# Branch A's projection by seven products of quarters, its operand sums by GpSimd in place, x added by accumulating DMA, the first half of the output projection by pairs of token blocks

## The chip, the cores and the metric

The kernel runs on one core of one Trainium2 chip. The core has five engines with queues of their own, each worked off in order: TensorE (PE in the profile; its weight loads are PEld), VectorE (DVE), ScalarE (ACT), GpSimd (POOL) and SyncE (SP). They wait for each other and for transfers through semaphores alone. The metric is the device time of one execution in microseconds (us); lower is better.

## The reference, cut to what matters

One decoder layer on 512 tokens of width 1024, in float32. The last part of it is touched:

```python
ya = ua * sa.reshape(bn, s_len, A_WIDTH) * jax.nn.silu(za)      # branch A, 512 x 1024
yb = o.reshape(bn, s_len, B_WIDTH) * jax.nn.silu(zb)            # branch B, 512 x 1024
merged = jax.nn.sigmoid(ga) * (ya @ w_branch_a[i]) + jax.nn.sigmoid(gb) * (yb @ w_branch_b[i])
mix_out = merged @ w_out[i]
ple = jax.nn.sigmoid(x @ w_ple_gate[i]) * (p[i] @ w_ple[i])
x = layer_norm(DEEPNORM_ALPHA * x + mix_out + ple, ln_g[i], ln_b[i])
```

## The kernel before

Every float32 operand of a matrix product is cut into a high part (the value rounded to float32r, by ScalarE) and a low part (the rest, by VectorE), and each product is three matmuls: high by high, high by low, low by high (`three`, L282). A matmul of the stages named here has a stationary tile of 128x128 and 512 columns (256 in the last block). `later(n, fn)` (L265) puts a piece of work on an agenda that is due n matmuls further on; `product` (L270) records a matmul and then everything due. So the order of work on each engine is written out by numbers counted in matmuls, and no engine holds a time. An engine runs ahead of its place in that order if its data are there.

Weights come as units of 512 KB through a ring of eight raw buffers `wr` (`pump`, L310). `high_part` and `low_part` (L399, L402) cut a unit into `wh` and `wl`, four buffers of each. After its low part, `follow` (L363) either frees the raw buffer, so that SP loads the next unit into it, or lets a GpSimd DMA add another unit to the raw buffer in place (`accum_op`, L375): so a sum of weight blocks is made.

`quad` (L640) computes a 512x1024 by 1024x1024 product as seven products of quarters instead of eight. Each of the seven is 24 matmuls (2 token blocks of 128 rows, 4 blocks of the inner dimension, 3 matmuls), 168 in all, and reads two units of weights or of weight sums; its left operands are quarters of x or yb and four sums of quarters. Between the products ScalarE copies partial results out of PSUM (`keep`, L649) and VectorE adds them (`block`, L653). `token_chunk` (L62) is the plain form: half of the columns, four token blocks side by side in four banks, 96 matmuls, four units.

The order of the stages at the end: gate of the embedding (quad "pg", 168 matmuls), embedding ("ple", 48), branch B's projection (quad "wb", 168, its weight sums for three of the seven products are made earlier in DRAM), **branch A's projection** ("wa", two calls of `token_chunk`, 192), output projection ("out", 192 matmuls for the first half of the columns in a `token_chunk` of 96 and for the second half block by block, 96 with the last token block in two halves). During "wa" the merge runs: the gate `ga` times the projection, plus `mb` (branch B's result times its gate), four transposes by TensorE into a bank (`merge_turn`, L1352), and a cut of that bank into `mh` and `ml`, the operand of "out". `residue` (L1276) loads x in eight pieces and VectorE adds ALPHA times x to `base`, which holds the embedding. `residual` (L1373) adds a bank of "out" to `base` and takes statistics; `last_norm` (L1378) normalises a token block and stores it.

Of the kernel before, what the change touches and what calls it, by code (L numbers as in the profile page):

```python
# [21 lines left out]
P = 128  # L22
D = 1024
T = 512
# [32 lines left out]
BEHIND = (8, 14)  # L57
GELU = 10
# [20 lines left out]
CUT_YB = (0, 4)  # L79
CUT_YA = (4, 8)  # L80
GATES_B = (14, 40, 56, 126)
RESIDUE = (32, 24)
# [28 lines left out]
def token_units(off):  # L111
    return [("t", off + c * T, kk) for c in range(2) for kk in range(4)]
# [23 lines left out]
def plan():  # L136
# [59 lines left out]
    add("wa", "a", token_units(0))  # L196
# [40 lines left out]
def hybrid_layer(ctx: ExitStack, tc: tile.TileContext, a, out: bass.AP):  # L237
# [185 lines left out]
    def next_pair(name, i):  # L423
        u = cursor[0]
        assert STEPS[u][0] == name, (STEPS[u][0], name)
        cursor[0] += 2
        for j in range(4):
            assert u + j in raw, (u, j)
        run(prep(u))
        run(prep(u + 1))  # L430

        pace = BLOCKS / 2 if name == "zq" else 1

        def ask(at, v, fits=lambda chain: True):
            if not pumping and v < len(STEPS) and fits(STEPS[v][2]):
                later(round(at * pace), lambda: run(load(v)))


        for v in range(u + 4, u + 8):
            ask(1, v, lambda chain: chain in ("x", "y"))  # L440
        within = [bool(v < len(STEPS) and STEPS[v][2]) for v in range(u, u + 6)]
        ask(1 if within[2] else 20, u + 6)
        ask(9, u + 5, lambda chain: chain != "b" and chain != "c")
        ask(12, u + 7, lambda chain: chain != "a" and (chain or within[4]))
        for j, at in enumerate(SPLITS.get(name, SPLITS[""])):

            at = BEHIND if i == 5 and j and name not in SPLITS else at
            spread(u + 2 + j, *(round(pace * n) for n in at))
        return split.pop(u), split.pop(u + 1)
# [185 lines left out]
    def operands(h, l, parts):  # L635

        s1, s2, n4, s3 = parts if callable(parts[0]) else [of_sum(parts, c) for c in range(4)]
        return (of_parts(h, l, 0, 0), of_parts(h, l, 4, 0), s1, n4, s2, s3, of_parts(h, l, 4, 2 * P))

    def quad(name, left, banks, place, done, last=None):  # L640
# [46 lines left out]
        for i, (bank, first, after) in enumerate(steps):  # L687
            w = next_pair(name, i)
            if i == 6 and last:
                last()  # L690
# [485 lines left out]
    def rstd_of(st):  # L1176
        mv = small([P, 2], "mv")
        dve.bn_aggr(out=mv, in_=st)
        dve.tensor_scalar(out=mv[:, 1:2], in0=mv[:, 1:2], scalar1=EPS, scalar2=None, op0=OP.add)  # L1179
# [82 lines left out]

    quad("pg", of_x, pairs(False), lambda c, t: base[:, t, c * T:(c + 1) * T], embedding_gate)
# [8 lines left out]
    def embed(c, t, bank):  # L1272
        z = base[:, t, c * T:(c + 1) * T]
        dve.tensor_tensor(out=z, in0=bank, in1=z, op=OP.mult)

    def residue(c, t):  # L1276
        z = base[:, t, c * T:(c + 1) * T]
        x = tmp[0]("x")
        sp.dma_start(out=x, in_=a["x"][t * P:(t + 1) * P, c * T:(c + 1) * T])
        later(20, lambda: dve.scalar_tensor_tensor(out=z, in0=x, scalar=ALPHA, in1=z,  # L1280
                                                   op0=OP.mult, op1=OP.add))

    ybh = big.tile([P, KT, T], F32R, name="ybh", tag="X0")
    ybl = big.tile([P, KT, T], F32R, name="ybl", tag="X1")
    ys = sum_tiles()

    def cut_yb(g, half):
        ts = slice(half * 2 * P, (half + 1) * 2 * P)
        cut(ybh[:, g, ts], ybl[:, g, ts], yb[0][:, g, ts])
# [3 lines left out]
    for i, (g, half) in enumerate([(g, 0) for g in range(KT)] + [(g, 1) for g in range(4, KT)]):  # L1293
        later(CUT_YB[0] + CUT_YB[1] * i, cut_yb, g, half)
    for i, c in enumerate((0, 2, 1, 3)):
        later(4 + 22 * i, load_sum, ys, ysd, c)
# [9 lines left out]

    ya = []

    def cut_ya(g):
        cut(ya[0][:, g, :], ya[1][:, g, :], ua[:, g, :])  # L1310

    def begin_ya():
        ya.extend(post.tile([P, KT, T], F32R, name=n, tag=tag) for n, tag in (("yah", "P0"), ("yal", "P1")))
        for g in range(KT):
            later(CUT_YA[0] + CUT_YA[1] * g, cut_ya, g)
# [11 lines left out]
    def load_gates_b(c, t, tag):  # L1327
        two = late.tile([P, 2, T], F32, name="two", tag=tag)
        gate["gb", c, t], gate["gb", c, t + 1] = two[:, 0, :], two[:, 1, :]
        sp.dma_start(out=two, in_=gates["gb"][t:t + 2, c].rearrange("t p n -> p t n"))  # L1330

    for i, (c, t) in enumerate(((0, 0), (1, 0), (1, 2), (0, 2))):
        later(GATES_B[i], load_gates_b, c, t, "gb"[i % 2])
    quad("wb", operands(ybh, ybl, ys), pairs(True), place_b, mb_done, begin_ya)
    for i in range(8):
        later(RESIDUE[0] + RESIDUE[1] * i, residue, i % 2, i // 2)

    lg = late.tile([P, D], F32, name="lg", tag="g")
    lb = late.tile([P, D], F32, name="lb", tag="b")
    later(100, sp.dma_start, lg, bcast(a["ln_g"], D))  # L1340
    later(130, sp.dma_start, lb, bcast(a["ln_b"], D))

    mh = big.tile([P, KT, T], F32R, name="mh", tag="X0")
    ml = big.tile([P, KT, T], F32R, name="ml", tag="X1")

    def merge(c, t, bank):
        m = gate.pop(("ga", c, t))
        dve.tensor_tensor(out=m, in0=bank, in1=m, op=OP.mult)
        dve.tensor_tensor(out=m, in0=m, in1=mb[0][:, t, c * T:(c + 1) * T], op=OP.add)
        later(12, merge_turn, c, t, m)  # L1350

    def merge_turn(c, t, m):  # L1352
        bank = pp() if c else pbank("sc", 2)
        for j in range(4):
# [3 lines left out]
        act.activation(mh[:, at[0], at[1]], turned, AF.Copy)  # L1358
        dve.tensor_tensor(out=ml[:, at[0], at[1]], in0=turned, in1=mh[:, at[0], at[1]].bitcast(F32),
                          op=OP.subtract)  # L1360
# [12 lines left out]
    def residual(t, piece, n, bank):  # L1373
        z = base[:, t, piece * n:(piece + 1) * n]
        dve.tensor_tensor(out=z, in0=bank, in1=z, op=OP.add)
        dve.bn_stats(out=zst[t][:, piece if n == T else piece - 1, :], in_=z)

    def last_norm(t, cuts):  # L1378
        mv, rs = rstd_of(zst[t])
# [9 lines left out]
    banks = other_banks()  # L1389
    token_chunk(banks, "out", mh, ml)  # L1390
    for t in range(NT):
        later(2 + 6 * t, residual, t, 0, T, banks[t])

    later(RETIRE, pool.drain)
    units = []
    for t in range(NT):
        ts = slice(t * P, (t + 1) * P)
        n = T if t < NT - 1 else T // 2
        for j in range(T // n):
            bank = pp()  # L1400
            for k in range(KT):
                if len(units) <= k // 2:
                    units.append(next_unit("out"))
                h, l = units[k // 2]
                m = slice((k % 2) * T + j * n, (k % 2) * T + (j + 1) * n)
                three(bank[:, :n], mh[:, k, ts], ml[:, k, ts], h[:, m], l[:, m], k == 0, k == KT - 1)
# [44 lines left out]
```

## Time and profile before

| what | us |
|---|---|
| median of three executions (620.26 to 621.1) | 620.74 |
| span of the profiled execution, first to last instruction | 618.3 |
| TensorE busy in that span | 610.0 |
| VectorE busy | 458.8 |
| ScalarE busy | 327.3 |
| GpSimd busy | 108.7 |

The profile gives the profiled execution's span, which is its own time from the first to the last instruction; what lies around it is the difference to the times, about 2.4 us. In a profile row, a group shows its line, engine, operation and tiles, then the count, busy us and mean ns of one, then the idle time before and what ended it. Waits of an engine that is not the last to be ready cost nothing.

### The profile page before, as it was taken

The numbers are of one execution on the slowest core, as the hardware profiler recorded it, in microseconds if no ns is written. First come the engines' busy times: TensorE is split into PE (matmuls) and PEld (weight loads), VectorE is DVE, ScalarE is ACT, GpSimd is POOL, SyncE is SP. The second block draws the span as 40 slices with busy tenths as digits, with TensorE's granted clock in tenths as the row PEclk, the third lists the DMA queues.
The fourth block names the chain that finished last, engine by engine and source line by source line (L and its number), as shares of the span: only waits on it lengthen the run. The fifth ranks groups of instructions, "written<-read, shape, count | busy, mean of one in ns | idle before, by whom it ended". The sixth has DMA issues, their size and how long they took to land.

```text
span 618.3 us, 8634 instructions
## 1 busy us (share of the span) xinstructions
PE 610.0 (99%) x3036; PEld 514.3 (83%) x3036; DVE 458.8 (74%) x800; ACT 327.3 (53%) x528; POOL 108.7 (18%) x120
## 2 busy tenths in 40 slices
PE   9999999999999999999999999999999999999995
PEld 6888888888888888888889988888888888888885
DVE  6996587878878866857578887677657659476486
ACT  6655664655645655478656765456567445232200
POOL 1234021332432620230102120111110010000011
PEclk9999999999999999999999999999999999999999
DMA  8689899679798598689898898999978997753002
GB/s 305 220 244 183 263 301 271 230 206 283 250 268 282 182 281 267 156 271 304 272 308 197 228 247 242 223 249 284 270 207 259 354 270 241 235 193 117 1 34 103
DMA packets 49888, 143.78 MB, mean 233 GB/s; under 512 B 6452, under 2 KB 7604, under 8 KB 49524
## 3 DMA queue, kind: packets, MB, share of 16 engines
q1 hardware_dynamic: 38772, 110.05, 50.4%
q0 software_dynamic: 8192, 28.58, 25.7%
q10 hardware_dynamic: 2880, 4.59, 2.0%
q8 instruction: 24, 0.39, 0.3%
q14 instruction: 20, 0.16, 0.1%
HBM read 120.00 MB, written 34.73 MB: 250 GB/s over the span
## 4 chain that ended last, share of the span: by engine, by line
PE 99%; DVE 0%; issue 0%; DVEq 0%
PE ps_pp L271 56%; PE ps_sc L271 18%; PE ps_tx L271 9%; PE ps_sc L821 3%; PE ps_po L866 3%; PE ps_po L271 3%; PE ps_tr L271 3%; PE ps_tr L855 1%; PE ps_po L475 1%; PE ps_tr L1208 1%; PE ps_po L1208 1%; PE ps_tx L905 0%; PE ps_sc L1355 0%; PE ps_pp L1355 0%; DVE base L1386 0%
## 5 line engine op out<-in xcount | busy, mean ns | idle before, releaser
L403 DVE TENSOR_TENSOR wl<-wr,wh 128x1024 fp32r<-128x1024 f32 (+1 forms) x136 | 166.4, 1227 | 53.8 <-ACT wh L400 53.1
L400 ACT ACTIVATE wh<-wr 128x1024 fp32r<-128x1024 f32 (+1 forms) x136 | 139.9, 1033 | 87.1 <-PE ps_po L271 15.6
L271 PE MATMUL ps_pp<-xh,wh 128*128 128x512 f32 (+1 forms) x276 | 109.5, 397 | 0.0
L271 PE MATMUL ps_pp<-xl,wh 128*128 128x512 f32 (+1 forms) x276 | 107.0, 388 | 0.0
L271 PE MATMUL ps_pp<-xh,wl 128*128 128x512 f32 (+1 forms) x276 | 105.4, 382 | 0.0
L834 ACT ACTIVATE p<-p,sth 128x128 f32<-128x128 f32 (+3 forms) x64 | 35.5, 556 | 47.3 <-DVE sth L832 47.2
L271 PEld LDWEIGHTS ps_pp<-xh,wl 128*128 128x128 f32 x276 | 52.0, 189 | 8.7
L271 PEld LDWEIGHTS ps_pp<-xh,wh 128*128 128x128 f32 x276 | 52.2, 189 | 8.4 <-ACT wh L297 0.5
L271 PEld LDWEIGHTS ps_pp<-xl,wh 128*128 128x128 f32 x276 | 52.2, 189 | 8.3 <-DVE xl L298 0.4
L375 POOL DMA_DIRECT2D wr<-in_w x26 | 22.6, 869 | 156.8 <-DVE wl L403 136.8
L828 DVE CUSTOM_DVE_ANT_0 p<-ps_sc,mask 128x128 f32<-128x128 f32 (+3 forms) x64 | 30.9, 483 | 5.6 <-PE ps_sc L821 5.6
L766 POOL TENSOR_TENSOR hl<-m,hl 128x512 fp32r<-128x512 f32 x16 | 25.1, 1609 | 54.7 <-ACT hl L761 54.7
L271 PE MATMUL ps_pp<-wh,xl 128*128 128x512 f32 x84 | 32.9, 391 | 0.0
L271 PE MATMUL ps_pp<-wl,xh 128*128 128x512 f32 x84 | 32.8, 390 | 0.0
L271 PE MATMUL ps_pp<-wh,xh 128*128 128x512 f32 x84 | 32.7, 389 | 0.0
L271 PE MATMUL ps_sc<-wh,xsh 128*128 128x512 f32 x80 | 31.2, 390 | 0.0
L271 PE MATMUL ps_sc<-wl,xsh 128*128 128x512 f32 x80 | 31.1, 389 | 0.0
L271 PE MATMUL ps_sc<-wh,xsl 128*128 128x512 f32 x80 | 31.1, 389 | 0.0
L1181 POOL TENSOR_TENSOR rs<-mv,mhalf 128x1 f32<-128x1 f32 x8 | 7.7, 961 | 121.6 <-DVE mv L1179 121.6
L271 PE MATMUL ps_pp<-wl,xsh 128*128 128x512 f32 x64 | 25.0, 391 | 0.0
L271 PE MATMUL ps_pp<-wh,xsl 128*128 128x512 f32 x64 | 25.0, 391 | 0.0
L271 PE MATMUL ps_pp<-wh,xsh 128*128 128x512 f32 x64 | 25.0, 390 | 0.0
(365 smaller groups left out, 1389.7 us busy)
## 6 DMA issues: line engine op xcount, KB each, us to landing
wr<-in_w SPq DMA_DIRECT2D x83, 512.0 KB, 4.7
wr<-in_w POOLq DMA_DIRECT2D x22, 512.0 KB, 6.1
k<-hl SPq DMA_DIRECT2D x16, 256.0 KB, 5.2
q<-hl SPq DMA_DIRECT2D x16, 256.0 KB, 4.3
ws_va<-in_w POOLq DMA_DIRECT2D x8, 512.0 KB, 10.9
wr<-ws_va SPq DMA_DIRECT2D x8, 512.0 KB, 4.3
wa<-in_w POOLq DMA_DIRECT2D x6, 512.0 KB, 7.3
kx<-hl SPq DMA_DIRECT2D x12, 256.0 KB, 5.8
```

The lines of the kernel that those rows point to most:

```text
L271: pe.matmul(ps, s, m, start=start, stop=stop, skip_group_check=read_within)
L375: pool.dma_start(out=raw[u][:, :n], in_=weights(STEPS[FOLLOWS[u]][1], n), accum_op=OP.add)
L400: act.activation(h, raw[u][:, :width(STEPS[u][0])], AF.Copy)
L403: dve.tensor_tensor(out=l, in0=raw[u][:, :width(STEPS[u][0])], in1=h.bitcast(F32), op=OP.subtract)
L475: pe.matmul(idle, zeros[:, :P], zeros, start=True, stop=True)
L766: pool.tensor_tensor(out=hl[:, 3 - j, :], in0=m[2 * j], in1=hl[:, j, :].bitcast(F32), op=OP.subtract)
L821: pe.matmul(sc[m][:, :n], q[:, m, i * P:(i + 1) * P], kk[:, m, :n], start=o == 0, stop=o == 1)
L828: dve.tensor_tensor_reduce(out=pr[m][:, :n], in0=sc[m][:, :n], in1=mask[:, T - n:], scale=-(DK ** -0.5), scalar=3e38, op0=OP.add, op1=OP.m ...
L834: act.activation(pr[m][:, :n], pr[m][:, :n], AF.Exp, bias=st[:, m:m + 1], scale=-1.0, accum_out=st[:, 2 + m:3 + m])
L866: pe.matmul(po[:, i * P:(i + 1) * P], at[:, j * P:(j + 1) * P], v[:, j, h * P:(h + 1) * P], start=j == 0, stop=j == i)
L1181: pool.tensor_tensor(out=rs, in0=mv[:, 1:2], in1=mhalf[:, 0:1], op=OP.pow)
L1208: pe.matmul(sa[:, t * P:(t + 1) * P], va[:, t, g * P:(g + 1) * P], aux[0][:, 0, g, :], start=True, stop=True)
```

## The change

**Branch A's projection becomes a `quad`.** It needs the quarters of ya (`ua`) as cut operands, and four sums of them. The sums are made in place: GpSimd subtracts and adds quarters of `ua` (`add_ya`, eight instructions of 128x2x256), and each quarter or sum is cut in two parts (`cut_ya`, 14 cuts in all). The weight sums of "wa" are all made by the chains of accumulating DMAs: eight in place of none, and 14 cuts of units in place of eight. The operands of "pg", "wb" and "wa" now share `xh`, `xl` and the sum tiles, quarter by quarter, as the stage before lets go of them; the sums of yb are loaded during "pg" instead of after it.

**The gates** of both branches are loaded in pairs into two slots of one tile. **x** is added to `base` by four accumulating DMAs of 512 KB on GpSimd's queue. To need no factor on x, `base` holds the sum divided by ALPHA (the embedding and "out" are scaled by 1/ALPHA as they are added; the constant in the norm is EPS / ALPHA ** 2).

**The merge** writes into the tile that `block` made; the addition of `mb` is on GpSimd for token blocks 0 and 1, on VectorE for 2 and 3; transposes go to the banks "tr" and "po". **The first half of "out"** runs token blocks 0 and 1 over all eight blocks of the inner dimension, and then 2 and 3, with four cut units held for both.

```diff
-CUT_YB = (0, 4)
-CUT_YA = (4, 8)
-GATES_B = (14, 40, 56, 126)
-RESIDUE = (32, 24)
+YA22, YA_S1, YA_S3, YA_CUT_S1 = (4, 35), (24, 60), (40, 76), (90, 97)
+YB11, YB12, YB22, LOAD_YS = (28, 43), (52, 59), (170, 177), (76, 100, 124, 148)
...
+GATES = (2, 14, 64, 142, 158, 192, 234, 308)
+OUT_FIRST, OUT_SECOND = (1, 5), (1, 3)
+LAST_NORM = (100, 130)
+MERGE = (24, 15)
+RESIDUE = (180, 36)
...
-    add("wa", "a", token_units(0))
+    quad("wa", "a", token_units(0))
...
+    def add_ya(to, op, x, y, part):
+        (z,), (x,), (y,) = (part_of((ua,), *q, part) for q in (to, x, y))
+        pool.tensor_tensor(out=z, in0=x, in1=y, op=op)
...
+    for n, c in zip(LOAD_YS, (0, 2, 1, 3)):
+        later(n, load_sum, ys, ysd, c)
     quad("pg", of_x, pairs(False), lambda c, t: base[:, t, c * T:(c + 1) * T], embedding_gate)
...
-        dve.tensor_tensor(out=z, in0=bank, in1=z, op=OP.mult)
-
-    def residue(c, t):
-        z = base[:, t, c * T:(c + 1) * T]
-        x = tmp[0]("x")
-        sp.dma_start(out=x, in_=a["x"][t * P:(t + 1) * P, c * T:(c + 1) * T])
-        later(20, lambda: dve.scalar_tensor_tensor(out=z, in0=x, scalar=ALPHA, in1=z,
-                                                   op0=OP.mult, op1=OP.add))
+        dve.scalar_tensor_tensor(out=z, in0=bank, scalar=1.0 / ALPHA, in1=z, op0=OP.mult, op1=OP.mult)
+
+    def residue(t):
+        pool.dma_start(out=base[:, t, :], in_=a["x"][t * P:(t + 1) * P, :], accum_op=OP.add)
...
+    for t in range(NT):
+        later(RESIDUE[0] + RESIDUE[1] * t, residue, t)
+    quad("wb", operands(xh, xl, ys), pairs(True), place_b, mb_done)
...
+    def merge(c, t, z, source):
+        dve.tensor_tensor(out=z, in0=source, in1=gate.pop(("ga", c, t)), op=OP.mult)
+        early = t < NT // 2
+        (pool if early else dve).tensor_tensor(out=z, in0=z, in1=mb[0][:, t, c * T:(c + 1) * T], op=OP.add)
+        later(MERGE[not early], merge_turn, c, t, z)
...
+        bank = pbank("tr" if t % 2 else "po", 1)
...
-    for c in range(2):
-        banks = main_banks() if c else other_banks()
-        for t in range(NT):
-            later(64 + 6 * t, load_gate, "ga", c, t)
-        token_chunk(banks, "wa", ya[0], ya[1])
-        for t in range(NT):
-            later(2 + 6 * t, merge, c, t, banks[t])
+    of_ya = [of_first_sum, of_sum(ys, 1), of_sum(ys, 2), of_sum(ys, 0)]
+    quad("wa", operands(xh, xl, of_ya, 0), pairs(False), lambda c, t: None, merge)
...
-        dve.tensor_tensor(out=z, in0=bank, in1=z, op=OP.add)
+        dve.scalar_tensor_tensor(out=z, in0=bank, scalar=1.0 / ALPHA, in1=z, op0=OP.mult, op1=OP.add)
...
-    banks = other_banks()
-    token_chunk(banks, "out", mh, ml)
...
+    for those in ((0, 1), (2, 3)):
+        banks = {t: pbank("sc", 2) for t in those} if those[0] else {0: pp(), 1: pbank("tx", 1)}
+        for k in range(KT):
...
+            for t in those:
+                ts = slice(t * P, (t + 1) * P)
+                three(banks[t], xh[:, k, ts], xl[:, k, ts], h[:, m], l[:, m], k == 0, k == KT - 1)
```

Three places show what it does to the order on the engines. The line numbers of rows of the changed program are its own: its L382 is L375 before (the accumulating weight DMA), its L410 is L403 (low part of a unit), its L278 is L271 (matmul). On GpSimd's queue, the end of the program before: `wr` with a number is a raw buffer, and the last two DMAs belong to "wb".

```order
L375 DMA wr_4017<-in_w 128x1024
L375 DMA wr_4096<-in_w 128x1024
L375 DMA wr_4685<-in_w 128x1024
L375 DMA wr_4733<-in_w 128x1024
L1181 TENSOR_TENSOR rs<-mv,mhalf 128x1 x4
```

The same queue in the changed program, from the middle of "wa" on: `base<-in_x` is x, and `s<-s,mb` the addition of the merge.

```order
L382 DMA wr_4829<-in_w 128x1024
L382 DMA wr_4858<-in_w 128x1024
L1387 TENSOR_TENSOR s_5090<-s_5090,mb 128x512
L1330 DMA base<-in_x 128x1024
L1387 TENSOR_TENSOR s_5110<-s_5110,mb 128x512
L382 DMA wr_4961<-in_w 128x1024
L382 DMA wr_4991<-in_w 128x1024
L382 DMA wr_4829<-in_w 128x1024
L1330 DMA base<-in_x 128x1024
L382 DMA wr_4858<-in_w 128x1024
L1387 TENSOR_TENSOR s_5262<-s_5262,mb 128x512
```

Where GpSimd had nothing from "wb" to the norms, it now issues weight sums, x and additions in one line; the last weight sum (`wr_4858`, second unit of the seventh product) stands behind the third piece of x.

On VectorE, the second half of "wa" before: a multiplication by the gate and an addition for each bank, with low parts of units between.

```order
L1348 TENSOR_TENSOR gate<-ps_pp,gate 128x512
L1349 TENSOR_TENSOR gate<-gate,mb 128x512
L1348 TENSOR_TENSOR gate<-ps_pp,gate 128x512
L1349 TENSOR_TENSOR gate<-gate,mb 128x512
L403 TENSOR_TENSOR wl<-wr_5122,wh 128x1024
L1359 TENSOR_TENSOR ml<-ps_pp,mh 128x4x128
```

The same engine in the changed program, from the seventh product's first low part: L663 is the sum of `block`, L1385 the gate, L1397 the low part of a turned bank.

```order
L410 TENSOR_TENSOR wl<-wr_4829,wh 128x1024
L1385 TENSOR_TENSOR s_5285<-s_5285,gates 128x512
L663 TENSOR_TENSOR s_5170<-s_5170,ps_pp 128x512
L410 TENSOR_TENSOR wl<-wr_4858,wh 128x1024
L1385 TENSOR_TENSOR s_5170<-s_5170,gates 128x512
L1387 TENSOR_TENSOR s_5170<-s_5170,mb 128x512
L1397 TENSOR_TENSOR xl<-ps_po,xh 128x4x128
L663 TENSOR_TENSOR s_5197<-s_5197,ps_pp 128x512
L1385 TENSOR_TENSOR s_5197<-s_5197,gates 128x512
L1387 TENSOR_TENSOR s_5197<-s_5197,mb 128x512
L410 TENSOR_TENSOR wl<-wr_5008,wh 128x1024
L1397 TENSOR_TENSOR xl<-ps_tr,xh 128x4x128
```

The merge of four banks, with the sums that the quarters need, now stands behind the low part of `wr_4858`.

On TensorE, the changed program in the middle of the seventh product: the transposes of two merged blocks stand between its matmuls.

```order
L278 MATMUL ps_pp<-wl,xh 128x512
L1393 MATMUL ps_tr<-ident,s_5285 128x128 x4
L278 MATMUL ps_pp<-wh,xl 128x512
L1393 MATMUL ps_po<-ident,s_5170 128x128 x4
L278 MATMUL ps_pp<-wh,xh 128x512
```

Before, the transposes of the first half of the columns stood among the matmuls of the second half, and those of the second half among the matmuls of "out".

More of the change, by code (lines that the diff above doesn't have):

```diff
@@ L57 @@
 BEHIND = (8, 14)
+LAST = (7, 11)
 GELU = 10
@@ L1335, in hybrid_layer @@
[L1335 to L1350, printed above, removed]
+    pairs_of_gates = late.tile([P, 2, 2, T], F32, name="gates", tag="R")
@@ L1352, in merge_turn @@
+    later(LAST_NORM[0], load_last, "ln_g", "g")
+    later(LAST_NORM[1], load_last, "ln_b", "b")
+    def merge(c, t, z, source):
[3 more added lines that the diff above has]
+        later(MERGE[not early], merge_turn, c, t, z)
     def merge_turn(c, t, m):
-        bank = pp() if c else pbank("sc", 2)
+        bank = pbank("tr" if t % 2 else "po", 1)
```

123 lines of the change are left out of this document (83 added, 40 removed).

## The prediction

> **What bounds the kernel now.** First I read the page's shares of busy time and its chain, then three stretches from the view by windows, cut at the start of branch B's projection, of branch A's, and of the output projection.
>
> ```profile
> PE 610.0 (99%) x3036; PEld 514.3 (83%) x3036; DVE 458.8 (74%) x800; ACT 327.3 (53%) x528; POOL 108.7 (18%) x120
> PE 99%; DVE 0%; issue 0%; DVEq 0%
> 482.10:520.20 38.10, 38.10 (x170) 31.55 (x169) 26.16 (x32) 19.46 (x23) 1.72 (x2) 1.00 0.91 293
> 520.20:565.60 45.40, 45.40 (x209) 37.62 (x209) 28.78 (x39) 13.38 (x17) 0.00 (x0) 1.00 0.63 214
> 565.60:618.30 52.70, 45.69 (x232) 38.63 (x230) 35.56 (x52) 7.59 (x9) 5.42 (x4) 0.98 0.10 41
> ```
>
> The windows' columns are the length, then busy us of PE, PEld, DVE, ACT and POOL, the granted clock, the DMA share and GB/s. TensorE is the bound: it works through all of the first two stretches, the chain that ends last is 99% its own, and the 7.0 us without it in the third are the last norm and store. So a matmul fewer is worth its full length, if nothing that TensorE now waits for comes late.
>
> **What goes.** The chain in order of time has a piece of 24 matmuls in a row, and it gives the borders of branch A's projection:
>
> ```profile
> 27.00 5.44 PE ps_tr L271 x24
> 517.47 2.72 PE ps_tx L271 x12
> 565.56 1.36 PE ps_sc L271 x6
> ```
>
> A matmul of 512 columns costs 5.44 / 24 = 0.2267 us. Branch A's projection goes from 192 of them to 168: 24 x 0.2267 = **5.44 us less**. Everything else on TensorE keeps its number: 32 transposes, 192 matmuls for the first half of "out" however its blocks are paired. In 520.19 to 565.56 lie 192 matmuls (43.5 us) and 16 transposes, so a set of four costs (45.37 - 43.5) / 4 = 0.46 us. The span would go from 618.3 to 612.9, and the median of 620.74 (2.4 us above the span, for what lies around it) to 615.3.
>
> **What is hidden.** VectorE gains ten cuts of ya in "wb" and loses none of its other work there; an instruction of that size costs 0.69 us, so 6.9 us beside 11.9 us that it has idle in the second window's 38.1. GpSimd's eight additions in place lie where it worked 1.7 us. The eight additions of x leave VectorE:
>
> ```profile
> L1280 DVE SCALAR_TENSOR_TENSOR base<-x,base 128x512 f32<-128x512 f32 x8 | 5.5, 685 | 1.9 <-DMA x<-in_x 1.9
> L907 DVE SCALAR_TENSOR_TENSOR yb<-ps_tx,g,yb x7: 739/750/751, 122.0 to 259.5; 128x512 f32<-128x512 f32 x7
> L1375 DVE TENSOR_TENSOR base<-ps_pp,base x5: 418/691/692, 594.7 to 611.3; 128x512 f32<-128x512 f32 x3, 128x256 f32<-128x256 f32 x2
> ```
>
> These 5.5 us were beside matmuls, so their going is worth nothing. The two-scalar form on a bank costs 0.75 in place of 0.69; behind the last matmul stands one of half the size, at most 0.06 us, which I leave out. The sums of yb (eight transfers of 512 KB) move into "pg". The most delicate transfer there is the last weight sum:
>
> ```profile
> 452.32 0.86 POOL L375 DMA_DIRECT2D wr<-in_w  x1 [0.94 <-DVE wl L403]
> DMA to landing us min/median/max: 6.2/6.2/6.2
> 462.62 1.04 ACT L400 ACTIVATE wh<-wr 128x1024 fp32r<-128x1024 f32 x1
> ```
>
> It landed at 458.5 and was used at 462.6: 4.1 us of cover. Two loads of 512 KB ahead of it cost 3.0 us (below), so I take nothing; without that cover it would be a stall of up to 2 us.
>
> **What is not hidden: the seventh product.** Count from the start of branch A's projection. After product n, TensorE is at 5.44 n, plus 0.46 for each set of transposes passed (after matmuls 63, 75, 137, 149, 150, 162). Two things meet there.
>
> *VectorE's line.* Its pitch, start to start, is shorter than its durations:
>
> ```profile
> 546.84 0.68 DVE L1348 TENSOR_TENSOR gate<-ps_po,gate 128x512 f32<-128x512 f32 x1
> 547.55 0.69 DVE L1349 TENSOR_TENSOR gate<-gate,mb 128x512 f32<-128x512 f32 x1
> 548.16 0.68 DVE L1359 TENSOR_TENSOR ml<-ps_sc,mh 128x512 fp32r<-128x512 f32 x1
> 591.19 1.21 DVE L403 TENSOR_TENSOR wl<-wr,wh 128x1024 fp32r<-128x1024 f32 x1
> 592.32 0.68 DVE L1375 TENSOR_TENSOR base<-ps_po,base 128x512 f32<-128x512 f32 x1
> 506.20 0.39 PE L271 MATMUL ps_pp<-wh,xsl 128*128 128x512 f32 x1
> 506.62 0.60 ACT L651 ACTIVATE s<-ps_pp 128x512 f32<-128x512 f32 x1 [1.66 <-PE ps_pp L271]
> ```
>
> The first number is the start, the second the duration. That is 0.71 after an instruction whose result is read, 0.61 after another, 1.13 after a low part; a copy out of PSUM starts 0.2 after the end of the last matmul's slot and takes 0.6. Product 5 ends at 27.2 + 0.92 = 28.1, its copy at 28.9. Then VectorE does the sum (28.9), the low part of unit 1 (29.5), a gate (30.65), a sum (31.3), and the low part of unit 2 at **31.9**. Call its start D. By the rows in the order, the bank "po" is free for the transposes after matmul 150 when the low part of the turned bank ends, at D + 1.13 + 0.71 + 0.61 + 0.69 = D + 3.1; those after matmul 162 wait for D + 6.9 (four instructions and a low part on); those in the first pair of "out" for the addition that ends at D + 10.0 (two more low parts, a turned bank, a gate). TensorE would reach the last of these, unhindered, at 172 x 0.2267 + 6 x 0.46 = 41.75. So its loss is D - 31.8 from D = 32 on: **0.1 us** with D = 31.9.
>
> GpSimd's addition of the merge, due at 31.35, lies beside that low part. The trace shows such a pair in the attention's stage, where GpSimd subtracts tiles of the same size:
>
> ```profile
> 57.90 2.87 POOL L766 TENSOR_TENSOR hl<-m,hl 128x512 fp32r<-128x512 f32 x2
> 59.41 2.44 DVE L403 TENSOR_TENSOR wl<-wr,wh 128x1024 fp32r<-128x1024 f32 x1 [2.37 <-ACT wh L400]
> L403 DVE TENSOR_TENSOR wl<-wr,wh x136: 948/1219/2445, 19.2 to 591.2; 128x1024 fp32r<-128x1024 f32 x122, 128x768 fp32r<-128x768 f32 x14
> ```
>
> The low part took 2.44 us instead of the median 1.22. I take it that VectorE waits out the 1.6 us addition: D = 33.0, a loss of **1.2 us**.
>
> *The weight sums.* Unit 2 is cut after the last accumulating DMA has landed, and ScalarE needs 1.05 for its high part, so D is at least the landing + 1.05. The rows in the order put five accumulating DMAs in one line ahead of it from the second piece of x on: x, two sums, one sum, x, and then this one. The trace has a line of four, the landings of its first and last, and the slowest pair:
>
> ```profile
> 50.92 0.86 POOL L375 DMA_DIRECT2D wr<-in_w  x1 [2.76 <-DVE wl L403]
> 52.05 0.86 POOL L375 DMA_DIRECT2D wr<-in_w  x1 [0.28 <-DVE wl L403]
> 55.54 0.85 POOL L375 DMA_DIRECT2D wa<-in_w  x1 [2.63 <-DVE wl L403]
> 57.34 0.86 POOL L375 DMA_DIRECT2D wa<-in_w  x1 [0.95 <-DVE wl L403]
> DMA to landing us min/median/max: 6.1/6.1/6.1
> DMA to landing us min/median/max: 7.5/7.5/7.5
> 386.89 0.86 POOL L375 DMA_DIRECT2D wr<-in_w  x1 [0.87 <-DVE wl L403]
> DMA to landing us min/median/max: 9.4/9.4/9.4
> q1 hardware_dynamic: 38772, 110.05, 50.4%
> q0 software_dynamic: 8192, 28.58, 25.7%
> ```
>
> The first landed at 57.0 and the last at 64.8: (64.8 - 57.0) / 3 = 2.6 us each. By the queues' shares of the 618.3 us, GpSimd's queue (q0) takes 25.7% x 618.3 / 28.58 = 5.56 us for a MB, 2.9 us for 512 KB; SP's queue (q1) takes 2.83 us for a MB, 1.5 us for 512 KB. GpSimd issues the second piece of x after the first addition of the merge, which waits for the bank of matmul 36 (8.2) and for VectorE's low part, sum and gate (to 10.9), and takes 1.6: 12.5. It lands 6.2 later, at 18.8. Five more at 2.6 to 2.9 put the last landing at 31.8 to 33.3, D at 32.9 to 34.4, the loss at **1.1 to 2.6 us**. Unit 1 of the same product lands two places earlier, at 26.6 to 27.5, and is cut at 28.1 or later: no loss.
>
> The two causes act on the same D, so they are not added. Between 1.1 and 2.6 I take **1.8 us**, the middle. Its ends for the range are 0 (neither holds) and 6.9 (below).
>
> The sum: -5.44 + 1.8 = -3.6 us; 618.3 becomes 614.7 in span, 620.74 becomes **617.1 us**.
>
> **The rivals.** *All of the gain.* If VectorE loses nothing beside GpSimd and the last sum lands before 30.9 (12.1 us for five, 2.4 each), the time is 615.3. For it: TensorE never waits in the stages before, with the same chains. Against it: the row of 2.44 and the pitch of 2.6.
>
> *Loads share the engines with the sums, and the kernel is slower.* Its place is the landing of the second unit of the seventh product. SP issues four transfers of 512 KB in the time of that line (a pair of gates, ln_g, two units): 4 x 1.5 = 5.9 us. If these go in turn with GpSimd's, the last landing is 31.8 + 5.9 = 37.7, D = 38.75, the loss 6.9 us, the time 620.74 - 5.44 + 6.9 = 622.2. It decides from a landing at 36.2 on (D = 37.25, loss 5.44), which is a pitch of (36.2 - 18.8) / 5 = 3.5 us. For it: the DMA of 386.89 took 9.4 us. Against it, in a stretch with transfers of both queues asked for, the shares of the queues:
>
> ```profile
> q0 software_dynamic: 97, 0.35, 107.1%
> q1 hardware_dynamic: 7, 0.02, 2.5%
> ```
>
> From 442 to 444 us GpSimd's queue had nearly all of the engines and SP's nearly nothing: the loads wait, not the sums. The Trainium skill says otherwise: its page "DMA: Bandwidth & Descriptors", section "SWDGE vs HWDGE vs iDMA", has each DMA engine take its queues in turn, GpSimd's and SP's being different ones. By that rule this rival would be the forecast; the trace of those 2 us does not agree with it, and no run here has both queues full for longer.
>
> *It doesn't do what it says.* The order has 24 rows fewer on TensorE, so the work does go; only waits can take it back.
>
> **How the numbers follow.** The forecast, with a loss from 0.6 to 4.2 us (615.9 to 619.5), has 0.62. All of the gain (below 615.9) has 0.20. The sums late (above 619.5) have 0.18: half of it within 0.2% of the time before, 619.5 to 622.0, which is about what a measurement of this kernel can tell from no change, and half slower. So faster 0.80 (forecast and all the gain, less 0.02 for its edge), same 0.11, slower 0.09. The range goes from 615.3, where there is nothing more to gain, to 620.8, which cuts off some 0.14 of the late cases and a little below.
>
> **What will show it.** The matmuls: the seven products at 38.1 us of TensorE's work, by windows; a longer stretch is waiting. The waits: in the view of waits, TensorE after VectorE at the three sets of transposes, some 1 to 2 us in all, in the seventh product and the first 16 matmuls of "out". VectorE: the low part of the last unit longer than 2 us would show GpSimd's part. The sums: landing times of GpSimd's DMAs of 6 us at first and some 10 for the last; ScalarE's high part of that unit waiting for a DMA. If TensorE waits in "pg", in "wb" or in the second half of "out", the covers above were wrong; if it waits nowhere, the time is 615.3; if the sixth and seventh products both wait for weights, the late case holds.

## The result, and the profile after

The changed kernel took **630.84 us** (median of four executions, 630.05 to 631.1) beside 620.55 us for the kernel before: the ratio is 1.0163, with a 95% interval of 1.0149 to 1.0177. It is slower by some 10 us, where 617.1 was forecast and 620.8 was the top of the range. The page of its profile, with the lines that answer to those shown of before:

```profile
span 629.1 us, 8655 instructions
PE 610.4 (97%) x3012; PEld 511.4 (81%) x3012; DVE 474.4 (75%) x800; ACT 337.9 (54%) x540; POOL 139.7 (22%) x144
...
PE 82%; DMA 7%; issue 5%; DVE 3%; ACT 1%; POOL 1%; DVEq 0%; POOLq 0%; ACTq 0%
```

The 24 matmuls are gone (3012 rows for 3036). But TensorE is idle for 18.7 us of the span instead of 8.3, and the chain that ended last, which was its own from end to end, now runs through DMA, other engines and the time to issue for a sixth of it. Its share of busy time, 97%, hides this; the busy time even includes matmuls at half the clock, as seen below.

The view by windows, cut where the first matmuls of branch B's projection, branch A's and the output projection start (columns: length, busy us and count of PE, PEld, DVE, ACT, POOL, then granted clock, DMA share, GB/s):

```profile
484.30:524.40 40.10, 38.89 (x170) 31.22 (x169) 33.42 (x36) 22.75 (x30) 9.70 (x8) 1.00 0.69 208
524.40:576.60 52.20, 44.95 (x193) 35.79 (x192) 32.45 (x37) 20.26 (x26) 15.20 (x15) 0.93 0.99 253
576.60:629.10 52.50, 45.11 (x226) 38.14 (x224) 33.23 (x48) 6.92 (x8) 5.57 (x4) 0.97 0.10 41
```

Branch A's projection starts at 524.4, where it was 520.2 before: **4.2 us are lost ahead of it**. It should take 168 x 0.2267 + 6 x 0.46 = 40.85 us of TensorE's work and takes 52.2: **11.3 us are lost in it**. Its DMA share went from 0.63 to 0.99, its granted clock from 1.00 to 0.93. The view of waits names TensorE's waits from "pg" to the end (us in total, times, longest):

```profile
PE ps_pp L278 <- ACT s L658: 4.6, 2, 3.2
PE ps_po L1393 <- DVE xl L1397: 3.4, 1, 3.4
PE ps_sc L278 <- DVE wl L410: 1.1, 1, 1.1
PE ps_po L1393 <- POOL s L1387: 0.6, 1, 0.6
PE ps_sc L278 <- ACT s L658: 0.2, 1, 0.2
```

Two waits in "pg" and "wb" (1.4 of the first row, and 1.1), and two long ones in branch A's projection: 3.2 us ahead of the sixth product, for a copy that stands on ScalarE behind a cut, and 3.4 us at the transposes after matmul 150. Before, TensorE waited nowhere there. In branch A's projection the waits make 7.2 of the 11.3 us, and the low clock behind the two long ones 3.2 (last section); ahead of it they make 2.7 of the 4.2 us. The rest is in gaps too short for this view. What is late is read from the chain of waits (start, us, what):

```profile
523.10 0.85 POOL wr L382
524.21 10.41 DMA wr<-in_w
534.70 1.07 ACT wh L407
535.79 1.24 DVE wl L410
537.32 7.88 DMA wr<-in_w
545.27 1.07 ACT wh L407
546.37 1.23 DVE wl L410
547.89 17.83 DMA wr<-in_w
565.80 1.07 ACT wh L407
```

That is one raw buffer: a sum by accumulating DMA, its cut by ScalarE and VectorE, the next sum into the same buffer, and so three times. The sums take 10.4, 7.9 and **17.8 us**; the median on the page of before was 6.1. The last lands at 565.7, 41.3 us into the stage; the prediction had 31.8 to 33.3. The DMA view from 523 to 566 us says why:

```profile
q0 software_dynamic: 1676, 6.14, 72.5%
q1 hardware_dynamic: 1853, 4.85, 32.8%
```

GpSimd's queue (q0) and SP's (q1) fill the 16 engines completely, and neither stands still for the other. Plain loads are late too: a pair of gates asked for at 529.6 took 16.4 us.

### The profile page after: what moved, and what is told of

The parts are those of the page before. It is cut to its first block, busy times and chain, and to the rows that moved or that the text cites. A ratio compares the mean times of both kernels' runs of the same rounds, so it can differ in the third digit from the quotient of the medians.

```text
span 629.1 us, 8655 instructions
## 1 busy us (share of the span) xinstructions
PE 610.4 (97%) x3012; PEld 511.4 (81%) x3012; DVE 474.4 (75%) x800; ACT 337.9 (54%) x540; POOL 139.7 (22%) x144
## 4 chain that ended last, share of the span: by engine, by line
PE 82%; DMA 7%; issue 5%; DVE 3%; ACT 1%; POOL 1%; DVEq 0%; POOLq 0%; ACTq 0%
PE ps_pp L278 51%; PE ps_sc L278 12%; DMA wr<-in_w 7%; PE ps_tx L278 7%; PE ps_sc L826 3%; PE ps_po L871 3%; PE ps_tr L860 1%; PE ps_po L278 1%; PE ps_tr L278 1%; DVE wl L410 1%; DVE xl L1276 1%; ACT wh L407 1%; POOL ua L1288 1%; PE ps_po L482 1%; PE ps_tr L1213 1%
## 5 line engine op out<-in xcount | busy, mean ns | idle before, releaser
L410 DVE TENSOR_TENSOR wl<-wr,wh 128x1024 fp32r<-128x1024 f32 (+1 forms) x143 | 178.7, 1254 | 46.9 <-ACT wh L407 46.4
L407 ACT ACTIVATE wh<-wr 128x1024 fp32r<-128x1024 f32 (+1 forms) x143 | 147.0, 1033 | 86.3 <-PE ps_sc L278 28.0
L278 PE MATMUL ps_pp<-xh,wh 128*128 128x512 f32 (+1 forms) x276 | 109.5, 397 | 0.0
L278 PE MATMUL ps_pp<-xl,wh 128*128 128x512 f32 (+1 forms) x276 | 107.0, 388 | 0.0
L278 PE MATMUL ps_pp<-xh,wl 128*128 128x512 f32 (+1 forms) x276 | 105.4, 382 | 0.0
L278 PE MATMUL ps_pp<-wl,xh 128*128 128x512 f32 (+1 forms) x168 | 64.6, 385 | 0.0
L278 PE MATMUL ps_pp<-wh,xh 128*128 128x512 f32 (+1 forms) x168 | 64.5, 384 | 0.0
L278 PE MATMUL ps_pp<-wh,xl 128*128 128x512 f32 (+1 forms) x168 | 64.5, 384 | 0.0
L278 PEld LDWEIGHTS ps_pp<-xh,wl 128*128 128x128 f32 x276 | 52.1, 189 | 8.7
L278 PEld LDWEIGHTS ps_pp<-xh,wh 128*128 128x128 f32 x276 | 52.1, 189 | 8.6 <-ACT wh L304 0.7
L278 PEld LDWEIGHTS ps_pp<-xl,wh 128*128 128x128 f32 x276 | 52.1, 189 | 8.2 <-DVE xl L305 0.4
L382 POOL DMA_DIRECT2D wr<-in_w x34 | 29.8, 875 | 126.4 <-DVE wl L410 113.8
L278 PEld LDWEIGHTS ps_pp<-wl,xh 128*128 128x128 f32 x168 | 32.0, 190 | 6.2 <-DVE wl L410 0.3
L278 PEld LDWEIGHTS ps_pp<-wh,xl 128*128 128x128 f32 x168 | 32.0, 191 | 6.0
L278 PEld LDWEIGHTS ps_pp<-wh,xh 128*128 128x128 f32 x168 | 31.9, 190 | 6.1
L278 PE MATMUL ps_pp<-wh,xsh 128*128 128x512 f32 x80 | 32.2, 402 | 4.6 <-ACT s L658 4.6
L278 PE MATMUL ps_sc<-wl,xsh 128*128 128x512 f32 x88 | 34.5, 392 | 1.2 <-DVE wl L410 1.1
L278 PE MATMUL ps_sc<-wh,xsh 128*128 128x512 f32 x88 | 34.5, 392 | 0.2 <-ACT s L658 0.2
L278 PE MATMUL ps_sc<-wh,xsl 128*128 128x512 f32 x88 | 34.3, 390 | 0.0
## 6 DMA issues: line engine op xcount, KB each, us to landing
ws_va<-in_w POOLq DMA_DIRECT2D x8, 512.0 KB, 10.5
```

The costliest lines, as they stand in the source:

```text
L278: pe.matmul(ps, s, m, start=start, stop=stop, skip_group_check=read_within)
L382: pool.dma_start(out=raw[u][:, :n], in_=weights(STEPS[FOLLOWS[u]][1], n), accum_op=OP.add)
L407: act.activation(h, raw[u][:, :width(STEPS[u][0])], AF.Copy)
L410: dve.tensor_tensor(out=l, in0=raw[u][:, :width(STEPS[u][0])], in1=h.bitcast(F32), op=OP.subtract)
```

## The experiments

Each row is the changed kernel with one edit or with several. "Start" is the first matmul of branch A's projection, "loss" its length less 40.85 us, both from the profiled execution, to within 0.3 us; "ratio" is to the kernel before on the same chip, with its 95% interval.

| kernel | start | loss | median us | ratio |
|---|---|---|---|---|
| before | 520.2 | - | 620.55 | 1 |
| changed | 524.4 | 11.3 | 630.84 | 1.0163 (1.0149 to 1.0177) |
| e1, x early | 525.8 | 4.8 | 627.14 | 1.0106 (1.0083 to 1.0129) |
| e2, sums of yb late | 523.3 | 11.3 | 629.39 | 1.0142 (1.0125 to 1.0160) |
| e3, sums of ya on VectorE | 521.3 | 10.5 | 627.50 | 1.0113 (1.0092 to 1.0133) |
| e4, x by plain loads | 524.7 | 7.0 | 627.19 | 1.0110 (1.0090 to 1.0130) |
| e5, x spread in "wb", e3 | 521.8 | 4.8 | 622.64 | 1.0035 (1.0024 to 1.0046) |
| e6, e5 and the merge on VectorE | 522.6 | 4.0 | 622.18 | 1.0025 (1.0014 to 1.0037) |
| e7, e6 and ln_g, ln_b late | 521.9 | 3.8 | 619.62 | 0.9994 (0.9972 to 1.0016) |
| e8, e7 with x behind the sums | 520.8 | 1.7 | 626.33 | 1.0102 (1.0086 to 1.0118) |
| e9, x behind the sums alone | 523.9 | 4.7 | 634.48 | 1.0230 (1.0208 to 1.0251) |
| e10, e7 with x last, by plain loads | 520.9 | 1.6 | 618.72 | 0.9974 (0.9964 to 0.9984) |
| e11, x last alone | 524.3 | 5.6 | 625.16 | 1.0074 (1.0060 to 1.0088) |
| e12, e10 with the merge on GpSimd | 520.6 | 2.1 | 619.58 | 0.9984 (0.9975 to 0.9993) |

**e1.** x's four accumulating DMAs at the start of branch B's projection.

```diff
-RESIDUE = (180, 36)
+RESIDUE = (16, 8)
```

> The four accumulating DMAs of x move from branch A's projection into the first 40 matmuls of branch B's. Theory 1 (one line of eleven accumulating DMAs, 3.5 us each, with three of x ahead of the last weight sum): that sum lands 3 x 3.5 = 10.5 us sooner, at some 31 us of the stage instead of 41.4; the two waits of 3.2 and 3.4 us and the low clock behind them go; the stage loses 1 to 2 us instead of 11.5, and the time is 620.5 to 623. Theory 2 (the weight sums are late by themselves, since each waits for VectorE to free its buffer, and x only fills the gaps): at most 3 us are won, 628 or more.

Theory 1 was right about the place and too generous about the size. The last sum landed at 560.1, 34.3 us into the stage (41.3 without the edit), and the loss there fell from 11.3 to 4.8. Less came back than expected, for two reasons. The sums of a buffer follow one another: two of them and their cuts stand ahead of the last, so that it was issued only 1.0 us sooner in the stage (22.5 us instead of 23.5). And x now disturbs "wb", where the view of waits has

```profile
PE ps_sc L278 <- DVE wl L410: 2.8, 2, 2.6
```

in place of 1.1: with x's four pieces landing after 6.5 to 12.7 us, SP's loads of the weight sums beside them took 8.4 to 13.8 us (3.5 to 5.8 in the changed kernel).

**e2.** The sums of yb are loaded after "pg".

```diff
-LOAD_YS = ... (76, 100, 124, 148)
+LOAD_YS = ... (172, 194, 216, 238)
```

> The sums of yb are loaded after the embedding's gate, as before the change (4, 26, 48, 70 matmuls into 'ple'). Theory 1 (these loads share the engines with the last weight sum of that stage, which lands 10.2 us after its issue instead of 5.5): it lands in 5 to 6 us, the wait of 1.4 us there goes and what follows it, 2.0 us in all: 628.5 to 629.2. Theory 2 (VectorE, held up by GpSimd's sums of ya, issues it 2.3 us late, and this alone is enough): the wait stays, 630.5 or more.

The wait of 1.4 us in "pg" went: the weight sum, issued no sooner, landed in 5.3 us. Branch A's projection started 1.1 us sooner. The median lies 0.2 us over the range of theory 1, and below theory 2; the intervals of the two ratios overlap, so that the times alone wouldn't show a gain of this size.

**e3.** `add_ya` on VectorE.

```diff
-        pool.tensor_tensor(out=z, in0=x, in1=y, op=op)
+        dve.tensor_tensor(out=z, in0=x, in1=y, op=op)
```

> The eight sums of ya in place are made by VectorE instead of GpSimd. If GpSimd's instructions hold up VectorE (instructions of 2.5 us for 0.7, 3.5 us for two low parts): the low part that was waited for in branch B's projection comes some 1 us sooner, the weight sum of the embedding's gate is issued some 2 us sooner, and both waits (1.4 and 1.1 us, 4 us with what follows) shrink: 627 to 629, though VectorE gets 8 x 0.7 us of its own. If VectorE is late there for its own number of instructions, 5.6 us more make it 631 to 633.

VectorE got eight instructions more and was less late: both waits went, branch A's projection started 3.1 us sooner, and the time fell by 3.3 us. So GpSimd's sums held VectorE up. In the changed kernel the rows of the two engines (start, duration) show it, first VectorE's, then GpSimd's:

```profile
441.99 0.68 DVE L663 TENSOR_TENSOR base<-ps_pp,s 128x512 f32<-128x512 f32 x1
442.59 2.54 DVE L1276 TENSOR_TENSOR xl<-ua,xh 128x512 fp32r<-128x512 f32 x1
```

```profile
442.95 1.62 POOL L1288 TENSOR_TENSOR ua<-ua 128x512 f32<-128x512 f32 x1
445.21 3.92 POOL L1288 TENSOR_TENSOR ua<-ua 128x512 f32<-128x512 f32 x2 [0.64 <-DVE xl L1276]
```

An instruction of 0.68 us takes 2.54 while GpSimd works; in e3, at 442.53, the same one took 0.68. The wait in "pg" thus needed both causes, and either edit removes it. The weight sum was issued at 452.85 instead of 450.52 in the kernel before, since VectorE was late (451.41 in e3), and landed after 10.2 us instead of 5.5, since the loads of yb's sums were beside it:

```profile
L382 POOL DMA_DIRECT2D wr<-in_w x1: 890/890/890, 452.9 to 452.9; - x1
...
DMA to landing us min/median/max: 10.2/10.2/10.2
```

**e4.** x by eight plain loads of SP at the places of before, added by VectorE.

```diff
-RESIDUE = (180, 36)
+RESIDUE = (32, 24)
...
+        sp.dma_start(out=x, in_=a["x"][t * P:(t + 1) * P, c * T:(c + 1) * T])
+        later(20, lambda: dve.tensor_tensor(out=z, in0=x, in1=z, op=OP.add))
```

> x comes as before the change by eight plain loads of SP, at the same places in branch A's projection, and VectorE adds it. If the number of places in GpSimd's line is what counts, the last weight sum lands 10.5 us sooner and the time is as with x early, 621 to 623. If the 16 engines are full and every byte counts, x still takes 4 x 1.45 of the 4 x 2.6 us: the last weight sum lands only some 4 us sooner and the time is 624 to 626. If x has no part in it: 630 or more.

The loss went to 7.0, between "changed" and e1, and the median is 1.2 us over the range of full engines. But x's bytes didn't make the sums late: the last one landed at 558.1, 33.3 us into the stage, 8 us sooner than in the changed kernel and no later than in e1 (34.3). So the place in GpSimd's line counts. What is left is on VectorE, which now adds x in the middle of the stage and works in order: ahead of the last two low parts it stood still for a load of x that took 6.6 us.

```profile
559.39 0.69 DVE L1333 TENSOR_TENSOR base<-x,base 128x512 f32<-128x512 f32 x1 [2.11 <-DMA x<-in_x]
```

The last low part started at 562.3, 37.6 us into the stage, though its sum had landed at 558.1, and TensorE had a new wait, 1.9 us for a sum by VectorE.

**e5, e6, e7.** Edits joined: x spread in "wb" with e3, then the merge's addition on VectorE, then the loads of ln_g and ln_b late.

```diff
-RESIDUE = (180, 36)
+RESIDUE = (12, 36)
...
-        (pool if early else dve).tensor_tensor(out=z, in0=z, ...
+        dve.tensor_tensor(out=z, in0=z, ...
...
-LAST_NORM = (100, 130)
+LAST_NORM = (150, 156)
```

> Two parts together: x added in branch B's projection, one piece each 36 matmuls from its 12th on (not four in a row), and the sums of ya by VectorE. If the two causes are separate ones, the 3.3 us won by VectorE's sums and the 6.7 us that x early won in branch A's projection add up, and the 1.5 us that the row of four pieces cost in branch B's projection do not come back: 620.5 to 622.5. If they overlap (the same wait counted twice), 624 or more.

622.64: the two gains added up, 0.1 us over the range. The pieces were not spread evenly, though: GpSimd runs ahead of the written order, and they started at 479.9, 481.3, 504.1 and 506.5 (e7's times; the order is the same in all three), the last two of them between and behind branch B's last sums.

> As the one with x spread and ya's sums on VectorE, and the merge's addition is on VectorE for all token blocks. If GpSimd's two additions hold VectorE up at the fourth product's low parts (3.5 us for two), the weight sums for the sixth product are issued some 2 us sooner, all four of the last row land 1.5 to 2 us sooner and the wait of 0.6 us at the first transposes goes: 618 to 620. If VectorE's own number of instructions sets these places: no gain, 621 to 623.

No gain that can be told apart (622.18, 620.75 to 624.25): the wait of 0.6 us went, and another of similar size came up in "wb". The expected 1.5 to 2 us did not come.

> As the one with the merge on VectorE, and the loads of ln_g and ln_b are asked for at matmuls 150 and 156 of branch A's projection instead of 100 and 130. If loads of SP's queue stretch GpSimd's line (3.5 us a piece with loads beside it, 2.5 without), the row of the last four weight sums is some 1 to 1.5 us shorter: 0.5 to 1.5 us below the one with the merge on VectorE. If the sums go ahead of the loads, as the prediction had it: the same within 0.5 us.

2.6 us faster, more than expected. But its profile has the last sum landing only 0.4 us sooner in the stage, so the line of the sums doesn't explain it; e6's profile has a wait of 0.8 us in "wb" that e7's lacks, and the executions scatter (620.75 to 624.25 and 618.25 to 625.76). What these loads cost is left open.

**e8, e9.** x behind the last weight sum in GpSimd's line, with e7's edits and alone.

```diff
-RESIDUE = (180, 36)
+RESIDUE = (292, 6)
```

> All four accumulating DMAs of x stand behind the last weight sum in GpSimd's line, where only the loads for the output projection are beside them; ya's sums and all of the merge are on VectorE, and ln_g and ln_b are loaded at matmuls 150 and 156 (as in the run with the norm's loads late). If x was still in the way of branch B's sums there (two pieces between them, landings of 9.4 us instead of 6), branch B's projection loses nothing and the weight sums of branch A's land no later than in that run: 617.5 to 619.5, below the kernel before. If x now holds up the loads for the output projection (four pieces of 2.6 us beside four loads), that stage loses 1 to 4 us: 620 to 623.

> The changed kernel with one edit: the four accumulating DMAs of x stand behind the last weight sum. If three places of x ahead of it cost 6.6 us in branch A's projection (as with x early, where it lost 4.8 us instead of 11.3), and branch B's projection stays as it was: 624 to 625. If the line is the whole of that loss, as the prediction's formula has it (last landing 10.5 us sooner): 620 to 622. If the places don't matter: 629 or more.

Both times went up (619.62 to 626.33 and 630.84 to 634.48), and they are the most instructive. Taken for itself, branch A's projection won as hoped: e9 loses 4.7 us in it instead of 11.3. In e8, branch A's projection is nearly clean. The windows (branch B's, branch A's, the rest):

```profile
482.10:520.70 38.60, 38.60 (x169) 31.31 (x168) 32.00 (x40) 22.75 (x30) 2.71 (x4) 1.00 0.69 217
520.70:563.20 42.50, 41.72 (x193) 33.74 (x193) 32.26 (x39) 20.59 (x26) 9.52 (x11) 1.00 1.01 241
563.20:624.10 60.90, 47.21 (x225) 39.54 (x224) 34.33 (x49) 6.81 (x8) 5.42 (x4) 0.91 0.22 83
```

The loss moved to the output projection, and the chain of e9 says to what:

```profile
561.75 0.33 SPq L367
...
562.13 14.79 DMA gates<-gate_ga
...
577.04 0.70 DVE z L1385
577.77 0.70 DVE z L1387
```

The last pair of gates is a plain load of 512 KB by SP. It took **14.8 us** beside three of x's pieces, 4.9 to 6.2 in the kernels without them there, and TensorE waited 8.2 us (6.4 in e8). So accumulating DMAs make loads late just as loads make them late. I had priced the loads for the output projection in e8's expectation, not the gates; the upper case there had 620 to 623, and 626.3 came. By its time e9 falls into its last case, 629 or more, but not for the reason given there: the places did matter in the stage, and the gates lost what it won.

**e10, e11.** x by plain loads, asked for behind the last gates and weights, added in the first half of the output projection; with VectorE's sums and merge and with ln_g and ln_b asked for after x (at matmuls 200 and 206), and alone.

```diff
-RESIDUE = (180, 36)
+RESIDUE = (152, 8)
...
+        later(36, lambda: dve.tensor_tensor(out=z, in0=x, in1=z, op=OP.add))
```

> x comes by eight plain loads of SP, asked for behind the last pair of gates and the last weights, and VectorE adds it during the first half of the output projection; ya's sums and all of the merge are on VectorE; ln_g and ln_b come after x. By theory 1 with its addition (accumulating DMAs and loads share the engines, so that each side is late when both are asked for): the stage of branch A loses 1.7 us as in the run with x behind, the last pair of gates lands in some 5 us instead of 10 to 15, and the wait of 6.2 us goes: 617 to 618.5, faster than the kernel before by 0.3% to 0.6%. If something else of the change holds the end up: 620 or more.

> The changed kernel with x alone altered: eight plain loads of SP behind the last gates, added by VectorE in the first half of the output projection; GpSimd keeps its sums of ya and its part of the merge. If x's four accumulating DMAs cost branch A's projection 6.6 us there and nothing else: 623.5 to 625. If GpSimd's part costs the 3.3 us that VectorE's sums of ya won, and the two add up with the merge's 0.6 and the norm's loads, this lies 5 to 7 us above the run with all of it.

e10 took 618.72 us, ratio 0.9974 (0.9964 to 0.9984): **faster than the kernel before**, 0.2 us over the top of the range expected. Its windows and all of TensorE's waits from "pg" on:

```profile
482.10:520.70 38.60, 38.60 (x170) 31.32 (x169) 32.02 (x41) 22.66 (x30) 2.60 (x3) 1.00 0.69 217
520.70:563.20 42.50, 41.61 (x194) 33.82 (x193) 32.41 (x40) 20.64 (x27) 6.08 (x7) 1.00 0.91 234
563.20:616.40 53.20, 45.30 (x226) 38.04 (x224) 38.88 (x57) 6.89 (x8) 5.42 (x4) 0.96 0.29 102
```

```profile
PE ps_po L1396 <- DVE xl L1400: 0.5, 1, 0.5
PE ps_tr L1396 <- DVE xl L1400: 0.4, 1, 0.4
PE ps_po L1396 <- DVE z L1390: 0.2, 1, 0.2
```

So the seven products do win time once the rest is out of their way: 1.9 us of span (616.4 for 618.3). e11, with x alone moved, took 625.16: a little above the range expected, and 6.4 us above e10, within the 5 to 7 us that the other edits were to add.

**e12.** e10 with the merge's addition on GpSimd for token blocks 0 and 1.

> As the run with x last, but the merge's addition for token blocks 0 and 1 is GpSimd's again. By the prediction's term (VectorE waits out GpSimd's addition beside a low part, 1.1 to 1.2 us, and all that stands behind it moves with it): the first transposes wait 0.6 us, two low parts take 3.5 us instead of 2.3, the weight sums of the last row start 1 us later: 619.5 to 621 against the 618.7 of the run with x last. If GpSimd's addition only takes work off VectorE there: 618.7 or less.

The hold-up is there, in VectorE's rows:

```profile
534.66 1.29 DVE L1388 TENSOR_TENSOR s<-s,gates 128x512 f32<-128x512 f32 x1
535.87 3.45 DVE L410 TENSOR_TENSOR wl<-wr,wh 128x1024 fp32r<-128x1024 f32 x2
```

Two low parts take 3.45 us together (2 x 1.13 by the pitch of before), and the loss of the stage is 2.1 us instead of 1.6. The median is 0.9 us higher, but the two were timed on different occasions, and their intervals overlap (0.9975 to 0.9993 and 0.9964 to 0.9984). So it costs about half a microsecond; more is not shown.

## Why the prediction was wrong, point by point

**5.44 us less matmul work: right.** 24 rows are gone. As time, the most that a kernel here keeps of it is 1.9 us (e10's span).

**"The loads wait, not the sums": this step failed.** It rested on two microseconds (442 to 444) in which GpSimd's queue had 107% and SP's 2.5%, and they were misread: SP had only the tail of a load to move there. Its two loads issued at 433.62 and 435.35 landed after 8.0 and 7.7 us, the later at 443.05, and the next was issued at 445.63. From 435.4 to 439.0, where both queues did have transfers under way (a sum issued at 429.8 landed at 439.0), the same profile of before has both of them served:

```profile
q1 hardware_dynamic: 236, 0.65, 47.1%
q0 software_dynamic: 73, 0.23, 32.6%
```

Over 43 us of the changed kernel, too, both were served: 72.5% and 32.8%. The rival by which loads and sums share the engines, given 0.18, was the mechanism. Its deciding point, a landing from 36.2 us on, was passed, and its sign came: the sixth and the seventh product both waited. From the second piece of x (landed at 548.4) to the last sum (565.7) there are five steps, 17.3 / 5 = 3.46 us. In that time GpSimd's queue had 79.1% of the engines and SP's 26.8%, so a step took 3.46 x 0.791 = 2.7 us of all engines: the price of 2.6 to 2.9 was right, and what failed is that the sums would have the engines to themselves. The Trainium skill's rule that the prediction set against the row (page "DMA: Bandwidth & Descriptors", section "SWDGE vs HWDGE vs iDMA": each DMA engine takes its queues in turn) agrees with these 43 us, and e9's load of 14.8 us shows the other half of it.

**The landing of the last sum, 31.8 to 33.3 us into the stage: 41.3 measured.** Of these 8.0 to 9.5 us, GpSimd issued the second piece of x at 15.3 instead of 12.5 (2.8 us), that piece took 8.7 us instead of 6.2 (2.5 us), and the five steps took 17.3 us instead of 13 to 14.5 (the rest). The first of these was a cause I hadn't counted: the line was not empty at its beginning, but held two sums and x's first piece, and the cut of those sums stands in ScalarE's and VectorE's order ahead of the merge. For the same reason the rival's price, 6.9 us, was too low.

**A loss of D - 31.8: right as a formula.** The low part of the last unit (D) started at 566.9, that is 42.5 us into the stage; the formula gives 10.7, and 11.3 was measured. The number agrees better than the path: the formula has TensorE wait last at the transposes in "out", for an addition that ended at 576.9, but TensorE, slowed behind its wait of 3.4 us, reached them only at 577.7.

**VectorE beside GpSimd, 1.2 us: right in kind, wrong in place.** I applied it only to the merge, where e12 puts it at about 0.5 us; the sign named for it, a last low part of over 2 us, did not come (1.2 us). I cost GpSimd's sums of ya at nothing, because GpSimd was free there; e3 puts them at 3.3 us, because VectorE was not free of them. Four of the eight don't even lie in the window of 1.7 us that I looked at, but in "pg". It was the same row (2.44 us for a low part) that should have been applied to all twelve of GpSimd's additions.

**Loads of yb's sums in "pg", hidden by 4.1 us of cover: failed.** The wait came at the sum ahead of the one that I had looked at. In the kernel before, that sum landed at 456.0 and its cut began at 459.8:

```profile
450.52 0.86 POOL L375 DMA_DIRECT2D wr<-in_w  x1 [7.99 <-DVE wl L403]
459.79 1.05 ACT L400 ACTIVATE wh<-wr 128x1024 fp32r<-128x1024 f32 x1
```

So it had 3.8 us of cover, and they were spent twice: 2.3 us by the late issue, 4.7 by the late landing. e2 and e3 each remove the wait. The text's price without the cover, up to 2 us, was about right: e2 won 1.4 us.

**x's leaving VectorE worth nothing, and its way in.** Nothing speaks against the first (in e10 VectorE adds x again, and no wait of TensorE comes from it); the second was not costed in full. Put behind the last gates as plain loads, x costs no wait that the profile shows (e10), while as accumulating DMAs in this stage it costs 5.7 us (e11 against the changed kernel).

**The low clock was not in the sum.** After each of the two long waits some eight matmuls ran at half speed (below), 3.2 of the 11.3 us. Not all of it is a price: the first spell lies ahead of the wait after matmul 150, which would have been longer by as much without it, since D set its end. The second made TensorE 0.8 us late for an addition in "out" that was done.

The count of 192 matmuls for the first half of "out" in the prediction should read 96; no term used it.

## What to carry to other kernels

A transfer taken off a compute engine has a price at the place where it lands: sum up the DMA time asked for in that stage by both queues, with the pitch of accumulating transfers, and where it comes to the stage's length, count on transfers of both queues being late (here 17.8 us for 6.1, and 16.4 for some 5). Which of them are late is set by the order in which they are asked for: with a DMA share of 1.01, e8 had the four last sums landing in 5.5 to 8.4 us, and the gates asked for after x took 13.0. Before a share of the engines is read as one queue going ahead of another, find out whether the other had transfers under way. Work for an idle engine isn't free if it holds up a busy one: look for a pair of rows that shows it, and apply it to each instruction that is moved. Slack that is measured once can be spent once: two edits that each fit into it may fail together.

## What the runs showed of the hardware that was not expected

*TensorE's clock after a wait.* The matmuls behind the wait of 3.2 us, in order of time (start, duration):

```profile
557.08 0.50 PE L278 MATMUL ps_pp<-wh,xsh 128*128 128x512 f32 x1 [3.21 <-ACT s L658]
...
558.86 0.63 PE L278 MATMUL ps_pp<-wh,xsl 128*128 128x512 f32 x1
559.29 0.63 PE L278 MATMUL ps_pp<-wh,xsh 128*128 128x512 f32 x1
559.71 0.63 PE L278 MATMUL ps_pp<-wl,xsh 128*128 128x512 f32 x1
```

From the fourth on they start every 0.43 us instead of 0.23, and the granted clock from 558 to 561 us is 0.50; some eight of them take 8 x 0.2 = 1.6 us more. This followed both waits of over 3 us in the changed kernel and in e2, one of two such in e3, and those of 6.4 and 8.2 us in e8 and e9; it followed none of the waits of up to 2.6 us. The Trainium skill's page "TensorE: Matmul & The Clock Gate" (section "Part 1: The HAM clock gate") has the array's clock halved after an idle window of some 3.4 us whose place is not tied to the program, and restored after a busy one; these runs agree in kind, the one wait of 3.2 us without it included; the other three waits of 3.2 us were followed by it, though they are a little shorter than that window.

*Two queues on the same engines.* An accumulating DMA of 512 KB landed 5.3 us after its issue where little was beside it (e10) and 17.8 us where both queues were full; a plain load of the same size took 3.1 us (e7) and 14.8 (e9), 16.4 in the changed kernel. In one place a first sum took 7.6 us (e7) and 5.5 and 5.3 (e8, e10); a load of gates lay beside it for 2.9 us in e7 and for 1.5 and 1.7 in the others, and whether that is all of the difference stays open.
